# Layer 1's attention projections cut from 512-column to 256-column products

## The chip, the cores and the metric

One core of a Trainium2 chip runs the whole program. The metric is the time of one execution on the device in microseconds (us), lower is better. The kernel before takes 557.86 us, the median of three runs (557.8 to 558.06).

## What is computed

Two transformer layers over 256 tokens of width 1024, in float32. Layer 0 mixes tokens by multi-head latent attention, layer 1 by block attention (with 256 tokens there is one block, so it is plain causal attention with a relative bias). Each is followed by an MLP with squared ReLU. Cut to what matters here:

```python
def moba_mixer(h, w_qkv, q_norm, k_norm, w_o, positions, rel_bias_table):
    B, S, _ = h.shape
    qkv = (h @ w_qkv).reshape(B, S, 3, MOBA_HEADS, MOBA_HEAD_DIM)   # 256 x 1024 times 1024 x 3072
    q = rms_norm(qkv[:, :, 0], q_norm).transpose(0, 2, 1, 3)
    k = rms_norm(qkv[:, :, 1], k_norm).transpose(0, 2, 1, 3)
    v = qkv[:, :, 2].transpose(0, 2, 1, 3)
    out = moba_attention(q, k, v, positions, rel_bias_table)
    return out.transpose(0, 2, 1, 3).reshape(B, S, MOBA_HEADS * MOBA_HEAD_DIM) @ w_o

# for i in range(DEPTH):
#     x = x + mixer(rms_norm(x, attn_norm[i]))
#     h = rms_norm(x, mlp_norm[i]);  a = relu(h @ w_in);  x = x + (a * a) @ w_out
```

## The kernel before

**Products in three parts.** Every large matrix product is made of three TensorE products of type float32r: high part times high part, low times high, high times low. Activations and weights are both split so. For the hidden state the parts are hTh and hTl, for the attention output aT0 and aT1, for the MLP's inner activations a0 and a1, for weights wh and wl. Heads and transposes are products of plain float32, the bias sums of layer 1 are bfloat16; the text calls both "of another type".

**Weights.** The weights come in 185 units of 128 x 1024 numbers, in one fixed order. SyncE loads a unit into one of four raw buffers, ScalarE casts it to wh (line 169), VectorE subtracts to get wl (line 178); wh and wl each have a ring of seven buffers. Units are split ahead of use by calls that stand by hand in the program: `hi` casts the next unit, `lo` makes the next wl, `fill` does one lo and then one hi. `done(i)` says that the program is past unit i. `hi` leaves its call out, without a word, where the unit would be more than seven ahead, and `lo` where there is no wh to work on; `unit(i)` makes up for what is missing at the moment it is asked for:

```python
    def hi(n=1, eng=nc.scalar):
            if i < min(used[0] + RING, len(units)):
    def lo(n=1, eng=nc.vector):
            if i < len(his):
    def unit(i):
        while len(los) <= i:
            lo()
    def done(i):
        used[0] = max(used[0], i + 1)
```

The order of the program is written by hand, and each engine runs its own instructions in that order.

**The projections of layer 1.** There are six names (k0, q0, v0, k1, v1, q1: key, query and value for heads 0 to 3 and 4 to 7), each with four units (k0 has units 89 to 92, q0 93 to 96, v0 97 to 100, and so on) and a result for each of two token tiles t. `proj1(name, t)` is one row of work: for each of eight k, three products with 128 columns of hTh or hTl standing still and 512 columns of wh or wl moving, 24 in all. k0 runs both t together, 48 products. Between rows stand transposes of finished tiles, and later the heads.

**The wide product.** In a stretch where products of another type came before, the next suitable product of the MLPs takes 258 columns in place of 256 (`wider`; the two more columns land beside the result and are not read). In the heads, `col(d, hh)` makes output row d of the attention's last projection, heads hh; there the product (d, h) = (5, 0) is the wide one. `run_heads` calls `col(4, ...)` in pieces between the heads, and rows 5 to 7 at the end.

Of the kernel before, what the change touches and what calls it, by code (L numbers as in the profile page):

```python
# [18 lines left out]
P = 128  # L19
# [4 lines left out]
S = 256  # L24
NT = S // P
KD = D // P
H = 8
# [33 lines left out]
def trunk(ctx: ExitStack, tc: tile.TileContext, A, out):  # L61
# [9 lines left out]
    def ps():  # L71
        return psum.tile([P, 512], F32, name="ps", tag="ps")
# [11 lines left out]
    def mm(o, a, b, start, stop):  # L84
        nc.tensor.matmul(o, a, b, start=start, stop=stop)  # L85

    def mm3(o, a, b, start, stop, wide=None, between=None):

        for i, (w, t) in enumerate(((0, 0), (1, 0), (0, 1))):
            if wide and i == 0:  # L90
                mm(wide[0], a[w], wide[1], start, False)
            else:
                mm(o, a[w], b[t], start and i == 0, stop and i == 2)
            if between and between[0] == i:
                between[1]()
# [7 lines left out]
    def wider(bank, b):  # L103
        moved[0] = True
        return bank[:, :S + 2], flat(b[:, :2])[:, :S + 2]
# [8 lines left out]
    def flat(ap):  # L114
        return ap.rearrange("p a b -> p (a b)")
# [20 lines left out]
    Q0 = len(units)  # L136
# [24 lines left out]
    def hi(n=1, eng=nc.scalar):  # L161

        for _ in range(n):
            i = len(his)
            if i < min(used[0] + RING, len(units)):
                load_raw()
                w = units[i][1]
                his.append(wsp.tile([P, 1024], F32R, name="wh", tag="wh"))
                (eng.copy if eng is nc.scalar else eng.tensor_copy)(his[i][:, :w], raws[i][:, :w])  # L169

    def lo(n=1, eng=nc.vector):

        for _ in range(n):
            i = len(los)
            if i < len(his):
                w = units[i][1]
                los.append(wsp.tile([P, 1024], F32R, name="wl", tag="wl"))
                eng.tensor_sub(los[i][:, :w], raws[i][:, :w], f32(his[i][:, :w]))  # L178
                load_raw()

    def fill(n=1):
        lo(n)
        hi(n)
# [7 lines left out]
    def unit(i):  # L191
        while len(his) <= i:
            hi()
        while len(los) <= i:
            lo()
        return his[i], los[i]

    def done(i):

        used[0] = max(used[0], i + 1)  # L200

    def part(u, sl):
        return u[0][:, sl], u[1][:, sl]
# [6 lines left out]
    x = const.tile([P, KD, S], F32)  # L210
# [72 lines left out]
    def hT(k, sl=slice(None)):  # L283
        return hTh[:, k, sl], hTl[:, k, sl]

    class SumSquares:


        def __init__(self):
            self.tot = work.tile([P, 2, S], F32, name="ssum", tag="ssum", bufs=1)  # L290
            self.prev = None
# [38 lines left out]
    class Norm:  # L330
# [19 lines left out]
        def rows(self, tok):  # L350
            self.y = t2(self.nh, self.width)
            nc.vector.scalar_tensor_tensor(self.y, self.p.rearrange("p (a b) -> p a b", b=self.width), tok,
                                           self.rs[:, :, None].to_broadcast([P, self.nh, self.width]),
                                           op0=OP.mult, op1=OP.mult)
# [201 lines left out]
    class Head:  # L556


        def __init__(self, hd, aT, h, bias, extra=None):
            self.aT = (aT[0][:, h], aT[1][:, h])  # L560
            self.two = aT[0][:, :2]
            self.i = h % HG
            self.hd = hd[h // HG]
            self.h, self.bias, self.extra = h, bias, extra
# [28 lines left out]
        def turn(self):  # L593
            pt = ps()
            for i in range(3):
                nc.tensor.transpose(pt[:, i * P:(i + 1) * P], self.p[:, i * P:(i + 1) * P], ident)  # L596
            self.pT = work.tile([P, 3 * P], F32, name="pT", tag="pT", bufs=3)
            nc.scalar.copy(self.pT, pt[:, :3 * P])
# [15 lines left out]
    def out_residual(a, d, gname):  # L614
        nc.vector.tensor_add(x[:, d], a, x[:, d])
        make_h_filled(d, gname)

    def run_heads(hs, proj, post, rows, turn, mid, base, gname, n1):

        A_ = [h.logits for h in hs]  # L620
        W_ = [h.weights for h in hs]
        B_ = [h.turn for h in hs]
        C_ = [h.values for h in hs]
        accs = []

        def o(h, ds=range(4)):
            u = unit(base + h // 2)
            for d in ds:
                if h == 0:
                    accs.append(ps()[:, :S])  # L630
                c = (h % 2) * 512 + d * P
                mm3(accs[d], part(u, slice(c, c + P)), hs[h].aT, h == 0, h == H - 1)
                if h == H - 1:
                    out_residual(accs[d], d, gname)
            if h % 2:
                done(base + h // 2)

        late = {}

        def col(d, hh):  # L640
            if d not in late:
                late[d] = ps()
            u = unit(base + d)
            for h in hh:
                mm3(late[d][:, :S], part(u, slice(h * P, (h + 1) * P)), hs[h].aT, h == 0, h == H - 1,
                    wider(late[d], hs[h].two) if (d, h) == (5, 0) else None)
            if hh[-1] == H - 1:
                done(base + d)
                out_residual(late[d][:, :S], d, gname)

        if mid is not None:
            proj("k1", 0)
            fill(n1)
            post("k1", 0)
            mid()
            proj("k1", 1)
            lo(n1)
            rows("k1", 0)
            hi(n1)
            post("k1", 1)  # L660
        A_[0]()
        proj("v1", 0)
        if mid is not None:
            lo(n1)
            rows("k1", 1)
        W_[0]()
        hi(n1)
        post("v1", 0)
        turn("k1", 0)
        A_[1]()  # L670
        if mid is None:
            rows("k1", 1)
        B_[0]()
        proj("v1", 1)
        lo(n1 + (mid is None))
        W_[1]()
        hi(n1)
        post("v1", 1)
        turn("k1", 1)
        C_[0]()  # L680
        A_[2]()
        B_[1]()
        proj("q1", 0)
        lo(n1)
        W_[2]()
        hi(n1)
        post("q1", 0)
        C_[1]()
        A_[3]()
        B_[2]()  # L690
        proj("q1", 1)
        lo(n1)
        W_[3]()
        rows("q1", 0)
        hi(n1)
        post("q1", 1)
        C_[2]()
        B_[3]()
        o(0)
        fill()  # L700
        turn("q1", 0)
        rows("q1", 1)
        C_[3]()
        o(1)
        fill()
        turn("q1", 1)
        o(2, range(2))
        A_[4]()
        o(2, range(2, 4))
        W_[4]()  # L710
        A_[5]()
        lo()
        o(3)
        B_[4]()
        hi()
        W_[5]()
        A_[6]()
        col(4, [0, 1])
        C_[4]()
        B_[5]()  # L720
        W_[6]()
        A_[7]()
        lo()
        col(4, [2, 3])
        C_[5]()
        B_[6]()
        hi()
        W_[7]()
        o(4)
        fill()  # L730
        C_[6]()
        B_[7]()
        o(5)
        fill()
        C_[7]()
        o(6)
        fill()
        col(4, [4, 5, 6])
        o(7)
        col(4, [7])  # L740
        for d in range(5, KD):
            col(d, range(H))
# [9 lines left out]
    open_p = {}  # L752
# [80 lines left out]
    heads_ctx, hd, aT = head_tiles(0)  # L833
# [16 lines left out]
    for o, a, b in rope_halves(m[:, :, 0], m[:, :, 1]):  # L850
        a, b = (i[:, :, None, :].to_broadcast([P, NT, 2, HALF]) for i in (a, b))
# [221 lines left out]
    for i, bs in enumerate(pairs):  # L1073
        at = 5 * i + 9
# [13 lines left out]
    order1 = {"k0": 0, "q0": 1, "v0": 2, "k1": 3, "v1": 4, "q1": 5}  # L1088
# [18 lines left out]
        tk = slice(t * P, (t + 1) * P)  # L1107
        to_T(norms[name, t].y, hd1[int(name[1])][name[0]][:, :, tk], gqk[:, 1:2] if name[0] == "q" else None)

    def proj1_k(name, t, p, k):  # L1110
        b = Q0 + 4 * order1[name]
        tk = slice(t * P, (t + 1) * P)
        mm3(p, hT(k, tk), part(unit(b + k // 2), slice((k % 2) * 512, (k % 2 + 1) * 512)), k == 0, k == KD - 1)

    def proj1(name, t):
        p = ps()
        for k in range(KD):
            proj1_k(name, t, p, k)
        if t == NT - 1:
            done(Q0 + 4 * order1[name] + 3)  # L1120
        open_p[name, t] = p

    for t in range(NT):
        open_p["k0", t] = ps()
    for k in range(KD):
        for t in range(NT):
            proj1_k("k0", t, open_p["k0", t], k)
        if k % 2:
            fill()
            done(Q0 + k // 2)  # L1130
    total = sums1[0].total()
    for t in range(NT):
        post1("k0", t, False)
    proj1("q0", 0)
    ss3 = small.tile([P, 1, NT], F32, name="ss3", bufs=1)
    tok_sums(ss3, [total], ps())
# [100 lines left out]
```

## Time and profile before

| what | value |
|---|---|
| median of three runs | 557.86 us |
| profiled execution, its own time | 557.87 us |
| its span (first to last instruction) | 556.1 us |
| TensorE busy (PE) | 551.3 us, 99% of the span |
| VectorE busy (DVE) | 394.4 us, 71% |
| ScalarE busy (ACT) | 303.3 us, 55% |
| granted clock of TensorE | 0.999 |

The span is what the profiler saw of the program; the 1.8 us between span and time lie around it. PE busy counts a product from its start to its modelled end, and ends overlap with the next start, so the pace of products is read from starts, not from busy time. The chain that ended last names the engine that was waited for: here TensorE holds 96% of it.

### The profile page before, as it was taken

To read this page: it belongs to the slowest core of one execution; us is meant where nothing else is said; L and a number is where in the kernel's file an instruction comes from. 1 tells how busy PE (TensorE), PEld (TensorE's weight loads), DVE (VectorE), ACT (ScalarE), POOL (GpSimd) and SP (SyncE) were. 2 spreads that over 40 slices of the span, in tenths; PEclk is the share of its full clock that TensorE was granted. 3 is DMA by queue.
4 is the path that set the end of the run, shared out by engine and by line. 5 is a ranking of instruction groups with operands and counts; after the bars stand their busy time and mean duration, and the time that the engine had idled before them with its cause. 6 is when DMAs were issued, how large, how long until landed. Compare 5 with 4: busy or idle time off the path is not lost.

```text
span 556.1 us, 10756 instructions
## 1 busy us (share of the span) xinstructions
PE 551.3 (99%) x4324; PEld 525.2 (94%) x4324; DVE 394.4 (71%) x654; ACT 303.3 (55%) x495; POOL 94.1 (17%) x108
## 2 busy tenths in 40 slices
PE   9999999999999999999999999999999999999997
PEld 7878999999999999999988888999999999999997
DVE  5997777687997689866668456767867653977630
ACT  6989675674533365435365465746856432655420
POOL 4892100032132000011133100000130311000100
PEclk9999999999999999999999999999999999999999
DMA  8833545586566466645456544453865764675810
GB/s 303 298 125 114 152 128 151 194 273 196 183 198 213 118 223 195 193 158 177 156 185 186 189 155 143 123 152 116 285 206 182 237 193 146 188 202 179 273 42 29
DMA packets 29186, 99.57 MB, mean 179 GB/s; under 512 B 3824, under 2 KB 4720, under 8 KB 29136
## 3 DMA queue, kind: packets, MB, share of 16 engines
q1 hardware_dynamic: 28656, 97.94, 55.4%
q0 software_dynamic: 336, 0.92, 0.4%
q8 instruction: 34, 0.56, 0.4%
q14 instruction: 16, 0.13, 0.1%
q10 hardware_dynamic: 144, 0.02, 0.0%
HBM read 97.82 MB, written 1.05 MB: 178 GB/s over the span
## 4 chain that ended last, share of the span: by engine, by line
PE 96%; DMA 2%; SPq 1%; issue 0%; DVE 0%; ACT 0%
PE ps L85 93%; PE ps L372 2%; DMA xs<-in_x_tok 1%; PE ps L596 1%; DMA win<-in_w_in 1%; SPq L158 0%; SPq L230 0%; PE ps L512 0%; DVE wl L178 0%; ACT wh L169 0%; DVE t L1063 0%; ACT sqj L477 0%; PE ps L879 0%
## 5 line engine op out<-in xcount | busy, mean ns | idle before, releaser
L178 DVE TENSOR_TENSOR wl<-raw,wh 128x1024 fp32r<-128x1024 f32 x177 | 218.3, 1249 | 34.5 <-ACT wh L169 33.9
L169 ACT CAST wh<-raw 128x1024 fp32r<-128x1024 f32 x177 | 182.8, 1047 | 71.7 <-PE ps L85 54.1
L85 PE MATMUL ps<-a,wh 128*128 128x256 f32 x1024 | 175.0, 276 | 0.0
L85 PEld LDWEIGHTS ps<-a,wh 128*128 128x128 f32 x1024 | 154.4, 188 | 0.0
L85 PE MATMUL ps<-hTl,wh 128*128 128x256 f32 x512 | 141.7, 277 | 0.0
L85 PE MATMUL ps<-a,wl 128*128 128x256 f32 x512 | 141.7, 277 | 0.0
L85 PE MATMUL ps<-hTh,wl 128*128 128x256 f32 x512 | 141.4, 276 | 0.0
L85 PE MATMUL ps<-hTh,wh 128*128 128x256 f32 x512 | 141.3, 276 | 0.0
L85 PEld LDWEIGHTS ps<-hTh,wh 128*128 128x128 f32 x512 | 96.1, 188 | 0.1
L85 PEld LDWEIGHTS ps<-hTl,wh 128*128 128x128 f32 x512 | 96.1, 188 | 0.1
L85 PEld LDWEIGHTS ps<-a,wl 128*128 128x128 f32 x512 | 96.1, 188 | 0.0
L85 PEld LDWEIGHTS ps<-hTh,wl 128*128 128x128 f32 x512 | 96.1, 188 | 0.0
L930 ACT ACTIVATE t<-ps 128x512 f32<-128x512 f32 (+1 forms) x34 | 19.5, 573 | 63.4 <-PE ps L85 63.4
L85 PE MATMUL ps<-aT,wh 128*128 128x256 f32 (+1 forms) x256 | 50.4, 288 | 0.0
L932 DVE SCALAR_TENSOR_TENSOR t<-ps,t 128x512 f32<-128x512 f32 (+1 forms) x34 | 22.4, 659 | 36.4 <-ACT t L930 36.2
L85 PE MATMUL ps<-wh,hTh 128*128 128x512 f32 (+2 forms) x128 | 46.5, 389 | 0.3 <-ACT wh L169 0.3
L85 PE MATMUL ps<-wl,hTh 128*128 128x512 f32 (+2 forms) x128 | 45.0, 377 | 0.1
L85 PE MATMUL ps<-wh,hTl 128*128 128x512 f32 (+2 forms) x128 | 44.8, 376 | 0.0
L85 PEld LDWEIGHTS ps<-aT,wh 128*128 128x128 f32 x256 | 40.4, 188 | 0.2
L85 PE MATMUL ps<-aT,wl 128*128 128x256 f32 x128 | 35.6, 278 | 0.0
L609 ACT ACTIVATE hTh<-x,gains 128x256 fp32r<-128x256 f32 x24 | 12.2, 510 | 42.3 <-POOL x L1054 25.8
L270 POOL TENSOR_TENSOR hrs<-hss,mhalf 128x4 f32<-128x4 f32 (+1 forms) x18 | 23.2, 1298 | 65.5 <-DVE hss L347 48.8
(167 smaller groups left out, 624.4 us busy)
## 6 DMA issues: line engine op xcount, KB each, us to landing
raw<-in_w_in_mlp SPq DMA_DIRECT2D x64, 512.0 KB, 4.3
raw<-in_w_out_mlp SPq DMA_DIRECT2D x64, 512.0 KB, 4.4
raw<-in_w_qkv SPq DMA_DIRECT2D x24, 512.0 KB, 4.0
raw<-in_w_u SPq DMA_DIRECT2D x8, 512.0 KB, 6.0
win<-in_w_in SPq DMA_DIRECT2D x8, 352.0 KB, 5.2
raw<-in_w_o0a SPq DMA_DIRECT2D x4, 512.0 KB, 3.9
raw<-in_w_o0b SPq DMA_DIRECT2D x4, 512.0 KB, 3.6
raw<-in_w_o1a SPq DMA_DIRECT2D x4, 512.0 KB, 4.0
```

The costliest lines, as they stand in the source:

```text
L85: nc.tensor.matmul(o, a, b, start=start, stop=stop)
L169: (eng.copy if eng is nc.scalar else eng.tensor_copy)(his[i][:, :w], raws[i][:, :w])
L178: eng.tensor_sub(los[i][:, :w], raws[i][:, :w], f32(his[i][:, :w]))
L270: nc.gpsimd.tensor_tensor(dst, t, mhalf[:, :n].rearrange("p (a b) -> p a b", b=t.shape[-1]) if len(t.shape) == 3 else mhalf[:, :n], op=OP.pow)
L372: nc.tensor.transpose(pt[:, i * P:(i + 1) * P], yf[:, i * P:(i + 1) * P], ident)
L596: nc.tensor.transpose(pt[:, i * P:(i + 1) * P], self.p[:, i * P:(i + 1) * P], ident)
L609: nc.scalar.activation(hTh[:, k], x[:, k], AF.Copy, scale=gain(gname, k))
L930: nc.scalar.activation(rl, src, AF.Relu)
L932: nc.vector.scalar_tensor_tensor(sq, src, 0.0, rl, op0=OP.max, op1=OP.mult)
```

## The change

`proj1` now runs a row through `proj1_row`. Each 512-column product becomes two of 256 columns with the same standing operand, 48 in a row (96 for k0). Of the two halves of one product, number (k, i) = (3, 1), the first is made 258 columns wide and put in the seventh place; the other has the 254 columns that are left, and goes to the end of the row. For k0 `done` is now called after 24 and after 96 products, where before it was called after each two k. In `run_heads` the wide product goes from (5, 0) to (4, 0) and (4, 5), in both layers.

```diff
-            self.two = aT[0][:, :2]
+            self.two = aT[0][:, h:h + 2] if h < H - 1 else None
...
-                    wider(late[d], hs[h].two) if (d, h) == (5, 0) else None)
+                    wider(late[d], hs[h].two) if d == 4 and h in (0, 5) else None)
...
-    def proj1_k(name, t, p, k):
-        b = Q0 + 4 * order1[name]
-        tk = slice(t * P, (t + 1) * P)
-        mm3(p, hT(k, tk), part(unit(b + k // 2), slice((k % 2) * 512, (k % 2 + 1) * 512)), k == 0, k == KD - 1)
+    def proj1_row(todo):
+        first = todo[0]
+        kick, rest = first[:2] + (3, 1, 0), first[:2] + (3, 1, 1)
+        todo = [x for x in todo if x not in (kick, rest)]
+        todo = todo[:6] + [kick] + todo[6:] + [rest]
+        last = {x[:2]: x for x in todo}
+        for x in todo:
+            name, t, k, i, half = x
+            c0, c1 = (0, S + 2) if x == kick else (S + 2, 2 * S) if x == rest else (half * S, (half + 1) * S)
+            w = unit(Q0 + 4 * order1[name] + k // 2)[i // 2][:, (k % 2) * 512 + c0:(k % 2) * 512 + c1]
+            mm(open_p[name, t][:, c0:c1], hT(k, slice(t * P, (t + 1) * P))[i % 2], w, (k, i, half) == (0, 0, 0),
+               x == last[name, t])
+            yield
...
-    for k in range(KD):
-        for t in range(NT):
-            proj1_k("k0", t, open_p["k0", t], k)
-        if k % 2:
+    row = [("k0", t, k, i, half) for k in range(KD) for t in range(NT) for i in range(3) for half in range(2)]
+    for at, _ in enumerate(proj1_row(row), 1):
+        if at % 24 == 0:
             fill()
-            done(Q0 + k // 2)
+            if at in (24, 96):
+                done(Q0 + at // 24 - 1)
```

What this does to the order on VectorE shows between the rows q0 and v0. The names are buffers: wl_3813, wl_3857 and wl_3903 are the low parts of units 98, 99 and 100; that of unit 97 was made earlier, while k0 ran. Before:

```order
L178 TENSOR_TENSOR wl_3813<-raw_3669,wh_3760 128x1024
L343 TENSOR_REDUCE hss_3820<-t2_3819 128x4
L347 TENSOR_SCALAR hss_3820<-hss_3820,sq3_3805 128x4
L352 SCALAR_TENSOR_TENSOR t2_3851<-ps_3692,rs_3_3803,hrs_3807 128x512
L352 SCALAR_TENSOR_TENSOR t2_3853<-ps_3693,rs_3_3803,hrs_3810 128x512
L352 SCALAR_TENSOR_TENSOR t2_3855<-ps_3771,rs_3_3803,hrs_3823 128x512
L178 TENSOR_TENSOR wl_3857<-raw_3722,wh_3817 128x1024
L343 TENSOR_REDUCE hss_3866<-t2_3865 128x4
L347 TENSOR_SCALAR hss_3866<-hss_3866,sq3_3805 128x4
L178 TENSOR_TENSOR wl_3903<-raw_3740,wh_3861 128x1024
```

In the changed kernel wl_3943, wl_3947, wl_3998 and wl_4014 are the low parts of units 97, 98, 99 and 100:

```order
L343 TENSOR_REDUCE hss_3882<-t2_3881 128x4
L347 TENSOR_SCALAR hss_3882<-hss_3882,sq3_3869 128x4
L352 SCALAR_TENSOR_TENSOR t2_3937<-ps_3692,rs_3_3867,hrs_3871 128x512
L352 SCALAR_TENSOR_TENSOR t2_3939<-ps_3693,rs_3_3867,hrs_3874 128x512
L352 SCALAR_TENSOR_TENSOR t2_3941<-ps_3811,rs_3_3867,hrs_3885 128x512
L178 TENSOR_TENSOR wl_3943<-raw_3639,wh_3877 128x1024
L178 TENSOR_TENSOR wl_3947<-raw_3669,wh_3879 128x1024
L343 TENSOR_REDUCE hss_3956<-t2_3955 128x4
L347 TENSOR_SCALAR hss_3956<-hss_3956,sq3_3869 128x4
L178 TENSOR_TENSOR wl_3998<-raw_3746,wh_3951 128x1024
L178 TENSOR_TENSOR wl_4014<-raw_3776,wh_3953 128x1024
```

Two low parts have moved from ahead of the three scalings of line 352 to behind them, so that all four units of v0 get theirs after these scalings.

On TensorE, this is the start of the first row of v0 in the changed kernel (the row's result is ps_3974):

```order
L85 MATMUL ps_3974<-wh_3877,hTh_156 128x256 [waits Activation_49]
L85 MATMUL ps_3974<-wh_3877,hTh_156 128x256
L85 MATMUL ps_3974<-wh_3877,hTl_157 128x256 x2
L85 MATMUL ps_3974<-wl_3943,hTh_156 128x256 [waits DVE_49]
L85 MATMUL ps_3974<-wl_3943,hTh_156 128x256
L85 MATMUL ps_3974<-wh_3879,hTl_157 128x258 [waits Activation_49]
L85 MATMUL ps_3974<-wh_3877,hTh_156 128x256 x2
L85 MATMUL ps_3974<-wh_3877,hTl_157 128x256 x2
L85 MATMUL ps_3974<-wl_3943,hTh_156 128x256 x2
```

The same place before:

```order
L372 MATMUL ps_3878<-ident_139,t2_3853 128x128 x4
L85 MATMUL ps_3884<-wh_3742,hTh_156 128x512
L85 MATMUL ps_3884<-wh_3742,hTl_157 128x512
L85 MATMUL ps_3884<-wl_3756,hTh_156 128x512
L85 MATMUL ps_3884<-wh_3742,hTh_156 128x512
L85 MATMUL ps_3884<-wh_3742,hTl_157 128x512
L85 MATMUL ps_3884<-wl_3756,hTh_156 128x512
L85 MATMUL ps_3884<-wh_3760,hTh_156 128x512
```

Each product has become two, the fifth of the row is the first that reads a low part, and the seventh is the wide one.

## Rows read from the trace of the kernel before

**Rows 1.** The page: engine, busy us (share of the span), instructions.

```profile
PE 551.3 (99%) x4324; PEld 525.2 (94%) x4324; DVE 394.4 (71%) x654; ACT 303.3 (55%) x495; POOL 94.1 (17%) x108
```

**Rows 2.** The chain in order of time, layer 1's projections: start us, us, what.

```profile
295.27 5.60 PE ps L85 x24
...
301.31 11.20 PE ps L85 x48
```

**Rows 3.** TensorE's timeline, layer 0's last output rows: start us, us, what.

```profile
80.71 0.36 PE L85 MATMUL ps<-aT,wh 128*128 128x256 f32 x1
80.91 0.28 PE L85 MATMUL ps<-aT,wl 128*128 128x256 f32 x1
...
84.80 0.28 PE L85 MATMUL ps<-aT,wl 128*128 128x256 f32 x1
```

**Rows 4.** TensorE's timeline, an MLP's second half, two of its products.

```profile
240.12 0.28 PE L85 MATMUL ps<-a,wl 128*128 128x256 f32 x1
...
244.88 0.28 PE L85 MATMUL ps<-a,wl 128*128 128x256 f32 x1
```

**Rows 5.** TensorE's timeline from a wide product of the MLP on.

```profile
131.73 0.28 PE L85 MATMUL ps<-hTh,wh 128*128 128x258 f32 x1
...
131.97 0.28 PE L85 MATMUL ps<-hTl,wh 128*128 128x256 f32 x1
...
132.54 0.28 PE L85 MATMUL ps<-hTh,wl 128*128 128x256 f32 x1
```

**Rows 6.** Groups by form on TensorE: the wide products, count, busy us, mean ns.

```profile
L85 PE MATMUL ps<-a,wh 128*128 128x258 f32 x4 | 1.1, 280 | 0.0
...
L85 PE MATMUL ps<-hTh,wh 128*128 128x258 f32 x3 | 0.8, 280 | 0.0
...
L85 PE MATMUL ps<-aT,wh 128*128 128x258 f32 x2 | 0.6, 280 | 0.0
```

**Rows 7.** TensorE's timeline where k0's row begins.

```profile
271.40 0.39 PE L85 MATMUL ps<-wh,hTh 128*128 128x512 f32 x1
...
272.33 0.40 PE L85 MATMUL ps<-wh,hTl 128*128 128x512 f32 x1
```

**Rows 8.** TensorE's timeline from the end of q0's first row to v0.

```profile
288.19 0.50 PE L85 MATMUL ps<-ones,ssum 128*128 128x2 f32 x4
...
294.24 1.03 PE L372 MATMUL ps<-ident,t 128*128 128x128 f32 x8
295.03 0.48 PE L85 MATMUL ps<-wh,hTh 128*128 128x512 f32 x1
```

**Rows 9.** VectorE's timeline there; in brackets its idle time before and the releaser.

```profile
294.46 0.75 DVE L352 SCALAR_TENSOR_TENSOR t<-ps,rs,hrs 128x512 f32<-128x512 f32 x1 [0.23 <-POOL hrs L270]
295.12 1.22 DVE L178 TENSOR_TENSOR wl<-raw,wh 128x1024 fp32r<-128x1024 f32 x1
296.26 0.68 DVE L343 TENSOR_REDUCE hss<-t 128x4 f32<-128x512 f32 x1
296.98 0.23 DVE L347 TENSOR_SCALAR hss<-hss,sq 128x4 f32<-128x4 f32 x1
297.11 1.22 DVE L178 TENSOR_TENSOR wl<-raw,wh 128x1024 fp32r<-128x1024 f32 x1
```

**Rows 10.** ScalarE's timeline at k0's end.

```profile
279.48 4.03 ACT L169 CAST wh<-raw 128x1024 fp32r<-128x1024 f32 x4
```

**Rows 11.** The chain in order of time, near the start: VectorE hands over to TensorE.

```profile
17.74 0.90 DVE wl L178
...
18.69 1.29 PE ps L85 x7
```

**Rows 12.** VectorE's timeline in the later rows, with its idle time.

```profile
313.17 0.69 DVE L343 TENSOR_REDUCE hss<-t 128x4 f32<-128x512 f32 x1 [5.86 <-ACT t L342]
...
320.62 2.35 DVE L178 TENSOR_TENSOR wl<-raw,wh 128x1024 fp32r<-128x1024 f32 x2
```

**Rows 13.** TensorE's timeline: v1's first row begins.

```profile
318.84 0.59 PE L85 MATMUL ps<-wh,hTh 128*128 128x512 f32 x1
```

More of the change, by code (lines that the diff above doesn't have):

```diff
@@ L1108, in turn1 @@
         to_T(norms[name, t].y, hd1[int(name[1])][name[0]][:, :, tk], gqk[:, 1:2] if name[0] == "q" else None)
-    def proj1_k(name, t, p, k):
-        b = Q0 + 4 * order1[name]
-        tk = slice(t * P, (t + 1) * P)
-        mm3(p, hT(k, tk), part(unit(b + k // 2), slice((k % 2) * 512, (k % 2 + 1) * 512)), k == 0, k == KD - 1)
+    def proj1_row(todo):
[11 more added lines that the diff above has]
+            yield
     def proj1(name, t):
-        p = ps()
-        for k in range(KD):
-            proj1_k(name, t, p, k)
+        open_p[name, t] = ps()
+        for _ in proj1_row([(name, t, k, i, half) for k in range(KD) for i in range(3) for half in range(2)]):
+            pass
         if t == NT - 1:
             done(Q0 + 4 * order1[name] + 3)
-        open_p[name, t] = p
     for t in range(NT):
         open_p["k0", t] = ps()
-    for k in range(KD):
-        for t in range(NT):
-            proj1_k("k0", t, open_p["k0", t], k)
-        if k % 2:
+    row = [("k0", t, k, i, half) for k in range(KD) for t in range(NT) for i in range(3) for half in range(2)]
+    for at, _ in enumerate(proj1_row(row), 1):
+        if at % 24 == 0:
             fill()
-            done(Q0 + k // 2)
+            if at in (24, 96):
+                done(Q0 + at // 24 - 1)
     total = sums1[0].total()
```

## The prediction

> **What bounds the kernel now.** I read the page first: TensorE is busy for 551.3 of 556.1 us [rows 1], so time is won only by a faster pace of its products, or lost by a wait put in front of it. Then the chain in order of time, for the pace of the part that is changed: 24 products of 512 columns take 5.60 us, 48 take 11.20, so 233.3 ns each, row after row [rows 2]. Then TensorE's timeline, start against start, for the pace of 256 columns. There are two. In the last rows of layer 0, behind the heads, 33 products lie between the two wl rows shown (of three products one reads wl): 84.80 - 80.91 = 3.89 us, 117.8 ns each [rows 3]. In the MLP 42 products lie between them: 4.76 us, 113.3 ns each [rows 4]. Same columns, same type, and a granted clock of 0.999 over the whole run. What changes the one pace into the other is seen at a wide product: it starts at 131.73, and from 131.97 to 132.54 five products take 0.57 us, 114 ns each [rows 5]. All nine wide products of the kernel [rows 6] are followed by the quick pace two products later; before them, back to the last product of another type, it is the slow one. So 512 columns cost 233.3 ns as one product, 226.7 as two quick ones, 235.6 as two slow ones.
>
> **Term 1, the projections' pace.** There are 288 products of 512 columns (k0 48, ten rows of 24), 67.2 us. They become 576. A single row starts behind transposes or heads, so slow: six products, then the wide one and the one after it, then 40 quick ones: 8 x 0.1178 + 40 x 0.1133 = 5.474 us against 5.600, a gain of 0.126; ten rows, 1.26 us. k0 follows the MLP's quick products directly, but the quick pace is gone at once when its operands come: four products from 271.40 to 272.33, 232.5 ns each [rows 7]. I treat it as a row that starts slow: 8 x 0.1178 + 88 x 0.1133 = 10.91 against 11.20, a gain of 0.29. Together -1.55 us. No row of before shows 256 columns with a weight moving and the hidden state standing, which is the reverse of the MLP. The bounds are therefore the two paces: 576 x 0.1133 = 65.3 us (-1.9) and 576 x 0.1178 = 67.9 (+0.7). I take the side of the quick one, because nine wide products of nine worked, with three different moving tiles; that they all had a weight standing is the reason to keep the other end.
>
> The Trainium skill speaks against this edit: TensorE: Matmul & The Clock Gate, Back-to-back issue gap, gives a product N / 2.4 + 2.5 ns at full clock, so that each of 288 products cut in two would pay another fixed 2.5 ns, an estimated 0.7 us more in all and nothing back. The trace agrees with neither of the levels that follow from it, 215.8 ns for 512 columns (measured 233.3) and 109.2 for 256 (113.3 or 117.8), but its fixed part is close to what two slow products cost over one, 2.3 ns.
>
> **Term 2, the wide product in the output rows.** From (4, 5) to the old place (5, 0) lie three products of head 5, three of head 6, twelve of `o(7)` and three of head 7: 21, all of type float32r, which go from 117.8 to 113.3 ns: 21 x 4.5 = 0.09 us, in two layers -0.19 us. The one at (4, 0) has five products behind it before heads of another type come: -0.02 us a layer at best; I count nothing.
>
> **Term 3, the weights come late.** k0's seventh product reads unit 90, whose other half is read last, so `done` for units 90 and 91 waits for the end of the row. Until then `hi` may go no further than unit 96. Before, k0's four `fill`s made wh and wl up to units 98 and 97; now the fourth does nothing. The next `fill(2)` casts 97 and 98, but its `lo`s find nothing to do, as wh and wl both stand at 96. So VectorE makes the low parts of 97 and 98 only at the `fill(2)` behind the three scalings of line 352, and those of 99 and 100 when v0's first row asks for them. ScalarE is no hurdle: before, it casts units 95 to 98 in one run up to 283.51 [rows 10], and even a few us later is in time.
>
> I set the clock at 288.19, the end of q0's first row [rows 8], since the norm's sums that follow feed VectorE's chain. The last scaling starts 6.27 us later, released by GpSimd (294.46) [rows 9]; this wait does not move. From there, with VectorE's own rows: scaling 0.66 (294.46 to 295.12), 97 and 98 1.14 each (295.12 to 296.26), reduction and scalar 0.85 (296.26 to 297.11), unit 99 1.22. Low part 97 is there after 6.27 + 0.66 + 1.22 = 8.15, 99 after 6.27 + 0.66 + 2.28 + 0.85 + 1.22 = 11.28 us. TensorE takes 0.05 us to start on VectorE's result (18.64 to 18.69) [rows 11].
>
> TensorE without a wait: sums and q0's second row 6.05 (to 294.24) less 0.13, transposes 0.79 (to 295.03): v0 starts at 6.71 [rows 8]. A first product of 256 columns behind another type takes 0.2 us to the next start (80.71 to 80.91) [rows 3]. The fifth product, which reads wl of unit 97, would start at 6.71 + 0.2 + 3 x 0.118 = 7.27 and waits until 8.20: 0.93 us. The 28th, first to read wl of unit 99, would start at 6.71 + 0.2 + 26 x 0.1135 = 9.86, and cannot before 11.33. The whole loss is the larger, **1.45 us**; 98 and 100 come 1.14 us after 97 and 99 and are asked for 13 and 12 products (1.4 us) after them, so add nothing. With the slow pace throughout v0 starts 0.15 later and reaches its 28th product at 10.1: 1.2 us. The bounds are 0 (if VectorE finds room earlier, for which I see no row) and 1.6. Behind the second wait 20 products may run slow, +0.05 us.
>
> No other row waits. k1: VectorE had 5.86 us of idle time there [rows 12]. v1: its low parts of 107 and 108 start where those of 108 and 109 do now, at 320.62 [rows 12]; 107 is ready at 321.9 and is read by the 28th product, no earlier than 318.84 + 0.2 + 26 x 0.1135 = 322.0 [rows 13]. That is the closest, 0.1 us to spare. By the attention's end both kernels have split the same units.
>
> **The sum.** -1.55 - 0.19 + 1.45 + 0.05 = -0.24 us on the profiled execution's 557.87 (its span 556.1 and 1.8 us around it; the median is 557.86): **557.6 us**, no change that can be told. A measurement of this kernel tells about 0.2%, 1.1 us, from no change.
>
> **The rivals.**
> - *The wait is not there* (12%): terms 1 and 2 stand alone, -1.74, 556.1 us. It decides for faster once the wait is under 0.6 us. It needs VectorE to finish unit 99 some 0.9 us earlier; the scaling that is released by GpSimd at 294.46 speaks against it.
> - *The quick pace does not come* (24%): with weights moving the wide product changes nothing, and 576 products at 117.8 ns cost +0.65; with the wait of 1.2 and the heads' -0.19 this is +1.66, 559.5 us, slower. It decides from a mean pace of 116.9 ns: 576 x 0.1169 - 67.2 + 1.2 - 0.19 = 1.1. For it: 512 columns in this arrangement never hold 226.7 ns; against it: nine of nine. The fixed part of the Trainium skill's page above leads to the same place: by its 2.5 ns, with wait and heads, an estimated 559.6.
> - *The quick pace comes in some rows, or ends at v0's wait* (14%): half of term 1's gain, -0.5 over all rows, + 1.35 - 0.19: about 558.5, still within 0.2%.
> - *The forecast* (50%): 557.2 to 558.1 by k0's row (-0.29 or +0.1) and the wait (1.2 to 1.6).
>
> So faster 0.13, same 0.63, slower 0.24. The range from 556.8 to 559.7 leaves out the first rival and a wait longer than I see; the forecast's own is 557.2 to 558.1.
>
> **What would show it.** Right: rows of 48 between transposes at about 5.47 us; starts 113 ns apart from the ninth product on; in v0's first row two idle times on TensorE of 0.9 and 0.5 us, released by VectorE's line 178; k0 near 10.9 us; rows 5 to 7 of the output unchanged, and the 21 products ahead of them at 113. Wrong: starts 118 apart behind the wide product (then 559.5), or no wait at v0 (then 556.1), or a wait in v1's first row too.

## The result, and the profile after

The changed kernel takes 565.51 us (median of four executions, 565.33 to 565.61) against 557.96 (557.80 to 558.82): a ratio of 1.0131, 95% interval 1.0118 to 1.0144. It is slower, and outside the predicted range. The page of the changed kernel (engine, busy us, share of the span, instructions), to set against [rows 1]:

```profile
span 563.8 us, 11328 instructions
...
PE 558.4 (99%) x4612; PEld 545.3 (97%) x4612; DVE 395.0 (70%) x654; ACT 302.0 (54%) x495; POOL 91.0 (16%) x108
```

TensorE has 288 products more, since 288 of 512 columns have become 576 of about half the width, and is busy 7.1 us longer. Where they lie shows in the chain of the changed kernel (start us, us, what); its pieces around layer 1's projections answer to [rows 2]:

```profile
79.25 215.10 PE ps L85 x1930
294.35 0.87 PE ps L372 x8
295.22 3.12 PE ps L85 x27
298.34 0.03 issue
298.37 2.74 PE ps L85 x21
...
301.55 11.14 PE ps L85 x96
...
364.41 196.15 PE ps L85 x1662
560.56 0.02 issue
```

and in the same places of the chain before:

```profile
78.89 215.50 PE ps L85 x1834
294.40 0.87 PE ps L372 x8
...
363.81 189.03 PE ps L85 x1662
552.84 0.02 issue
```

The two chains read against each other give the whole difference of 7.72 us in the spans. Up to 79 us the changed kernel is 0.36 late, a delay that is there at 18 us, ahead of any changed instruction. From there to the end of q0's second row it wins 0.41 (the heads' edit in layer 0, k0 and q0's first row). To 364 us it loses 0.65, some 0.45 in the other rows and 0.2 in layer 1's heads. The last piece then loses 7.12. It holds 1662 products in both kernels: 189.03 / 1662 = 113.7 ns each before, 196.15 / 1662 = 118.0 after. That is the slow pace of [rows 3] from layer 1's last heads to the end of the program, where before the quick one of [rows 4] began at 369.95. The granted clock is 1.0.

The two wide products that should have ended it ran and did not. In the second MLP, whose code the change does not touch, the wide product behind the norm's sum stands in TensorE's timeline of the changed kernel as in [rows 5], with the opposite effect:

```profile
418.15 0.59 PE L85 MATMUL ps<-ssum,ones 128*128 128x256 f32 x2
...
419.05 0.28 PE L85 MATMUL ps<-hTh,wh 128*128 128x258 f32 x1
419.17 0.28 PE L85 MATMUL ps<-hTh,wl 128*128 128x256 f32 x1
...
419.87 0.28 PE L85 MATMUL ps<-hTh,wl 128*128 128x256 f32 x1
```

From 419.17 to 419.87 lie six products, 117 ns each. [Rows 5] had 114 there.

The slow pace has a beat. Three slow products take 353 ns, which the trace gives as 117, 118 and 118, and one of each three has a duration 1 ns longer than the other two (the ends are modelled, so this is a mark of how the starts fall, no more). Groups by line and form show which one it is: count, shortest, median and longest duration in ns, first and last start. Ahead of the wide product that worked in the kernel before (369.95), the long one is always the product that reads wl, the second of each three:

```profile
L85 PE MATMUL ps<-aT,wh x23: 279/279/279, 365.9 to 369.8; 128*128 128x256 f32 x23
L85 PE MATMUL ps<-aT,wl x12: 280/280/280, 365.8 to 369.7; 128*128 128x256 f32 x12
```

Ahead of the one that failed in the changed kernel (368.09) it is never wl, but one of the two that read wh (by single products the first: 280 at 367.73, then 279 at 367.85 and 367.97):

```profile
L85 PE MATMUL ps<-aT,wh x9: 279/279/280, 366.6 to 368.0; 128*128 128x256 f32 x9
L85 PE MATMUL ps<-aT,wl x5: 279/279/279, 366.4 to 367.9; 128*128 128x256 f32 x5
```

So the long product lies two before the wide one that worked, and three before the one that failed. At 419.05 it lies one before. That is the **theory of the beat**: in a slow stretch a wide product works only when the long one lies two before it. The rivals: the **place** (4, 5) or its two columns are wrong and (5, 0) is right; or the **projections**' new form leaves something behind.

### The profile page after: what moved, and what is told of

Read it like the earlier page. It is cut to its first block, busy times and chain, and to the rows that moved or that the text cites. A ratio compares the mean times of both kernels' runs of the same rounds, so it can differ in the third digit from the quotient of the medians.

```text
span 563.8 us, 11328 instructions
## 1 busy us (share of the span) xinstructions
PE 558.4 (99%) x4612; PEld 545.3 (97%) x4612; DVE 395.0 (70%) x654; ACT 302.0 (54%) x495; POOL 91.0 (16%) x108
## 4 chain that ended last, share of the span: by engine, by line
PE 96%; DMA 2%; SPq 1%; issue 0%; DVE 0%; ACT 0%
PE ps L85 93%; PE ps L372 1%; DMA xs<-in_x_tok 1%; PE ps L596 1%; DMA win<-in_w_in 1%; SPq L158 0%; SPq L230 0%; PE ps L512 0%; DVE wl L178 0%; ACT wh L169 0%; DVE t L1064 0%; ACT sqj L477 0%; PE ps L880 0%
## 5 line engine op out<-in xcount | busy, mean ns | idle before, releaser
L85 PE MATMUL ps<-a,wh 128*128 128x256 f32 x1024 | 178.5, 278 | 0.0
L85 PE MATMUL ps<-wh,hTh 128*128 128x256 f32 (+2 forms) x224 | 46.3, 291 | 0.9 <-ACT wh L169 0.9
L85 PE MATMUL ps<-wh,hTl 128*128 128x256 f32 (+2 forms) x224 | 46.7, 285 | 0.0
L85 PE MATMUL ps<-wl,hTh 128*128 128x256 f32 (+2 forms) x224 | 45.2, 286 | 0.1
L85 PEld LDWEIGHTS ps<-wh,hTh 128*128 128x128 f32 x224 | 34.8, 189 | 1.8 <-ACT wh L169 1.2
L85 PEld LDWEIGHTS ps<-wh,hTl 128*128 128x128 f32 x224 | 35.5, 188 | 0.0
```

## The experiments

All are compared with the kernel before, run on the same chip in the same job (medians 558.3 to 558.4).

**Which part?** *heads_only* is the kernel before with the line of `col` changed and the projections as they were; *proj_only* is the changed kernel with the wide product back at its old place.

```
-  self.two = aT[0][:, :2]      # heads_only
+  self.two = aT[0][:, h:h + 2] if h < H - 1 else None
...
-  wider(late[d], hs[h].two) if (d, h) == (5, 0) else None)
+  wider(late[d], hs[h].two) if d == 4 and h in (0, 5) else None)
```

> The kernel before with the wide product of the output rows moved to (4, 0) and (4, 5) and nothing else. Beat theory (a wide product turns the slow pace into the quick one only on one of three places in the slow pace's beat): (4, 5) lies 21 products, seven beats, ahead of (5, 0), so it hits as (5, 0) did, unless the changed layer 0 moves the beat; about 557.7 us, and layer 1's MLP at 113.3 ns a product. Place theory (moving the wide product is itself what loses layer 1's MLP): about 565 us.

> The changed kernel with the wide product of the output rows back at (5, 0). Beat theory: what comes ahead of layer 1's output rows is that of the changed kernel, and (5, 0) has the same place in the beat as (4, 5), so it misses too and layer 1's MLP stays at 117.8 ns: about 565.5 us. Place theory: the MLP is quick again, about 558.3 us.

*proj_only* takes 565.42 (ratio 1.0130, 1.0115 to 1.0145): all of the loss, with the wide product at its old place. That ends the rival of the place. *heads_only* takes 557.73 to 558.97 in nine executions and 565.44 in one, the profiled one: the same program makes both times, which neither rival allows. Its profile has the failing beat ahead of the wide product:

```profile
L85 PE MATMUL ps<-aT,wh x9: 279/279/280, 366.4 to 367.8; 128*128 128x256 f32 x9
L85 PE MATMUL ps<-aT,wl x4: 279/279/279, 366.6 to 367.7; 128*128 128x256 f32 x4
```

Its instructions in layer 1 are those of before up to the wide product at 357.41, so the two can be followed to the first gap that differs. It is that of the first output product behind a head's logits in layer 1: it lasts 469 ns in the kernel before (first fence) and 467 in *heads_only* (second), while the gaps between the 800 products ahead of it agree to 1 ns.

```profile
L85 PE MATMUL ps<-aT,wh x1: 469/469/469, 353.2 to 353.2; 128*128 128x256 f32 x1
```

```profile
L85 PE MATMUL ps<-aT,wh x1: 467/467/467, 353.6 to 353.6; 128*128 128x256 f32 x1
```

Where the last stretch begins, behind the last head's values, the first product lasts 362 ns in the kernel before (first fence) and 365 in *heads_only* (second), and from there on the long one stands elsewhere:

```profile
L85 PE MATMUL ps<-aT,wh x1: 362/362/362, 365.6 to 365.6; 128*128 128x256 f32 x1
```

```profile
L85 PE MATMUL ps<-aT,wh x1: 365/365/365, 366.1 to 366.1; 128*128 128x256 f32 x1
```

This holds in all fourteen traces: where this product lasts 365 ns (nine traces, the changed kernel's among them), the long product is then the first of each three; where it lasts 362 or 363, it is the second (four traces), or there is no slow pace (one, *own_early0* below). A shift of 3 ns at an entry decides over 7 us.

**The same wide product, one or two products later.** In the changed kernel layer 1's wide product at (4, 5) becomes the second (*beat1*) or the third (*beat2*) of its three.

```
-            if wide and i == 0:
-                mm(wide[0], a[w], wide[1], start, False)
+            if wide and i == (wide[2] if len(wide) > 2 else 0):
+                mm(wide[0], a[w], wide[1], start and i == 0, stop and i == 2)
...
+                if n1 == 2 and h == 5:            # layer 1, (4, 5); beat1: hs[h].two) + (1,)
+                    return wider(late[d], hs[h].two1) + (2,)
```

> The changed kernel, in layer 1 alone the 258 columns at (4, 5) taken by the second of its three products (low weights) in place of the first. Beat theory: in the changed kernel's slow stretch the first product is one place late against the stretches where it hit, the second is two late; it misses again, about 565.5 us (or some 5 less if the MLP's own wide product at its sums happens to hit). Place theory: no difference from the changed kernel, 565.5 us.

> The changed kernel, in layer 1 alone the 258 columns at (4, 5) taken by the third of its three products (low part of the attention output moving). Beat theory: this is the place that hits; quick from there to the end of the program, 6.8 us of the MLP and 0.3 of the output rows back: about 558.4 us. Place theory, or something that the projections leave behind (ring, instruction fetch): no difference, 565.5 us.

*beat2* takes 558.44 in the median of ten executions (558.00 to 558.96; ratio 1.0003, 0.9993 to 1.0013): two products' delay gives back all 7 us, with the projections of the changed kernel, so these leave nothing behind that keeps the pace slow by itself. The beat at the entry is that of the changed kernel, and the third product has the long one two before it:

```profile
L85 PE MATMUL ps<-aT,wh x10: 279/280/280, 366.2 to 367.7; 128*128 128x256 f32 x10
L85 PE MATMUL ps<-aT,wl x5: 279/279/279, 366.4 to 367.8; 128*128 128x256 f32 x5
```

*beat1* takes 560.40 (ratio 1.0040, 1.0024 to 1.0056): the second product misses, but the MLP's own wide product, at 419.21, now works and the quick pace holds from there.

**The MLP's own wide product.** *sums_earlier* is the changed kernel with the norm's sum one product earlier in layer 1, to put the wide product a product later behind it.

```
-  between = other_type(1, lambda: mm(pb[:, :S], ones, s, True, True))
+  between = other_type(0 if l else 1, lambda: mm(pb[:, :S], ones, s, True, True))
```

> The changed kernel, with the norm's sum of layer 1's MLP one product earlier, so that its wide product (missed at 419.05 us) comes fifth instead of fourth behind the sum's row. Theory of the beat (of three slow products one lasts 1 ns longer, and a wide product works when that one lies two before it, as in every one that worked): in the changed kernel the long one was the last before the wide product, so it now lies two before. It works, 1196 products go from 117.8 to 113.3 ns, 5.4 us: 560.1. Rival, the MLP cannot be made quick after a missed wide product in the heads, or its operands no longer fit: nothing changes, 565.5. A third way, the new place of the sum shifts the beat again: also 565.5, and the durations ahead of the wide product tell it from the rival.

565.38 (ratio 1.0121, 1.0101 to 1.0142): nothing gained. The durations are 280, 279, 279 ahead of the wide product, so the beat moved with the sum, the third way of the expectation. A beat read in one version does not hold in the next.

**The control on the kernel before.** *heads_third* is *heads_only* with layer 1's wide product on the third product.

> The kernel before the change with its output rows' wide product at (4, 0) and (4, 5) (558.2 in nine executions, 565.4 in one), in layer 1 on the third product of (4, 5) instead of the first; the projections are those of before. Theory of the beat: where the first falls on it, the third doesn't: it now misses in most executions and works in few, the reverse of the other kernel. Missed, layer 1's output rows and MLP stay slow, 560.2 if the MLP's own wide product works, 565.4 if not. Rival (the third of three is simply the better place, since it worked in all ten executions with the changed projections): 558.2 in all.

The median is 565.06 (ratio 1.0092, 1.0065 to 1.0119): six of ten executions take 565.1 to 565.8, three 559.4 to 560.1, one 557.84. *heads_only* had nine of ten near 558. The third product is not the better place as such. The profiled execution is the one at 557.84, and has the beat of *beat2*.

**A wide product in a quick stretch.** *undo* is the kernel before with a second wide product in each layer, 24 products behind the one that works.

```
-  wider(late[d], hs[h].two) if (d, h) == (5, 0) else None)
+  wider(late[d], hs[h].two) if (d, h) in ((5, 0), (6, 0)) else None)
```

> The kernel before the change, with one more wide product in each layer, at (6, 0) of the output rows, 24 products behind the one at (5, 0), where the pace is quick already. Theory (a wide product in a quick stretch turns it slow): in both layers the pace is 113.3 from (5, 0) on, 117.8 from (6, 0) on, until the wide product behind the next sums: some 375 products x 4.5 ns = 1.7 us in each layer, 558.3 + 3.4 = 561.7, if the wide products there still fall on the beat; if layer 1's misses, its 1196 products add 5.4, 567.1. Rival (a wide product sets the quick pace whatever it was, and what ended it in the projections' rows is that weights move): no change, 558.3.

561.66 (ratio 1.0060, 1.0042 to 1.0077), as expected. Groups ahead of the added wide product of layer 1, and behind it:

```profile
L85 PE MATMUL ps<-aT,wh x15: 276/276/276, 372.3 to 374.7; 128*128 128x256 f32 x15
L85 PE MATMUL ps<-aT,wl x7: 276/276/276, 372.5 to 374.6; 128*128 128x256 f32 x7
...
L85 PE MATMUL ps<-aT,wh x18: 279/280/281, 375.0 to 378.0; 128*128 128x256 f32 x18
L85 PE MATMUL ps<-aT,wl x9: 279/279/281, 374.9 to 377.8; 128*128 128x256 f32 x9
```

276 is the quick pace's duration, 279 and 280 the slow one's: the wide product does not set a pace, it changes it.

**The rows without it.** The same happens in the projections. In the changed kernel seven of the eleven rows have turned quick by themselves when their seventh product comes; it is the wide one, and turns them slow. q0's first row seems to start slow for a like reason: it follows k0 directly, which is quick up to its last product, the one of 254 columns, and slow from that one on (starts 113 or 114 ns apart before, 117 to 119 after, in all ten traces with the new rows). No run leaves that product alone out. *own_pace* is *beat2* with wide products only in k0, q0's and v0's first row and k1's first; *own_pace2* leaves out k1's too.

```
-        kick, rest = first[:2] + (3, 1, 0), first[:2] + (3, 1, 1)
...
+        kick = rest = None
+        if first[:2] in (("k0", 0), ("q0", 0), ("v0", 0), ("k1", 0)):   # own_pace2: without k1
+            kick, rest = first[:2] + (3, 1, 0), first[:2] + (3, 1, 1)
...
```

> The changed kernel with layer 1's wide product at (4, 5) on its third product (558.4), and without a wide product in the seven rows where it ended a quick pace that was there already: q0's and v0's second row, k1's second, both of v1 and both of q1; their 48 products have 256 columns each. Theory (a row behind transposes or heads turns quick by itself within five products, and the wide product in a quick stretch turns it slow): these rows go from 5.72 to about 5.48 us, seven times -0.24, -1.7: 556.7, provided that the wide product at (4, 5) still falls on the beat; if it doesn't, some 6.8 more, 563.5, with the rows quick all the same. Rival (the pace of a row falls back by itself a few products on, as with 512 columns): rows of 48 x 117.8 = 5.7 us, no change, 558.4.

> As own_pace (557.4: wide product at (4, 5) on its third product, none in the seven rows that turn quick by themselves), and none in k1's first row either: there the row before is quick to its end, so k1's row begins quick and the wide product turned it slow (5.63 us). Theory: k1's first row 5.44 us, -0.19: 557.25, if the wide product at (4, 5) still works. Rival (the entry into the output rows shifts with the shorter row, as with the early splits): the third product misses, 563; or part of the executions each way.

*own_pace*: 557.44 (ratio 0.9981, 0.9972 to 0.9990); *own_pace2*: 557.20 (0.9980, 0.9971 to 0.9989). Both are 0.2% faster than the kernel before, and none of their executions (ten and eleven) is above 557.94; a miss costs 2 us (*beat1*) or more, so all kept the quick pace to the end. TensorE's timeline of q0's second row, the changed kernel first, then *own_pace*:

```profile
289.01 0.39 PE L85 MATMUL ps<-wl,hTh 128*128 128x256 f32 x2
289.24 0.28 PE L85 MATMUL ps<-wh,hTl 128*128 128x258 f32 x1
289.35 0.40 PE L85 MATMUL ps<-wh,hTh 128*128 128x256 f32 x2
...
293.83 0.40 PE L85 MATMUL ps<-wl,hTh 128*128 128x256 f32 x2
```

```profile
289.18 0.39 PE L85 MATMUL ps<-wh,hTh 128*128 128x256 f32 x2
...
293.71 0.40 PE L85 MATMUL ps<-wl,hTh 128*128 128x256 f32 x2
```

From 289.35 to 293.83 lie 38 products, 118 ns each; from 289.18 to 293.71 in *own_pace* 40, 113 each. The two products ahead of the wide one at 289.24 take 0.23 us, 115 ns each, so the row was quick already. The seven rows gain 0.18 us each, not the 0.24 that I expected, 1.26 in all. Of that 0.25 goes into v0's first row, which begins earlier and waits longer (5.90 us in *beat2*, 6.15 here), and 0.14 into k1's first, which now begins quick and was turned slow by its wide product; *own_pace2* has that back (5.63 to 5.44). That its time is the expected one is in part luck: q1's first row, which has no wide product in either, turned quick in *own_pace* and stayed slow through all its 48 products in *own_pace2* (5.54 and 5.74 us). Its products of high part times high part, by durations, first *own_pace*, then *own_pace2*:

```profile
L85 PE MATMUL ps<-wh,hTh x16: 276/276/369, 333.3 to 338.3; 128*128 128x256 f32 x16
```

```profile
L85 PE MATMUL ps<-wh,hTh x16: 281/281/365, 333.0 to 338.2; 128*128 128x256 f32 x16
```

The same row stayed slow in *own_early* and *own_early0*. All rows together are only 0.05 us shorter in the trace of *own_pace2* than in that of *own_pace*, and their two ratios do not differ clear of noise.

**v0's wait.** *early* is *beat2* with units 97 and 98 split behind k0's row; *own_early* has *own_pace*'s rows too; *own_early0* has *own_pace2*'s rows and the wide product at (4, 5) on its first product.

```
     for t in range(NT):
         post1("k0", t, False)
+    both(2)
     proj1("q0", 0)
```

> The changed kernel with the wide product at (4, 5) on its third product (558.4), and units 97 and 98 cast and split right behind k0's row instead of three rows later. Theory (v0's first row waits 0.2 us for the low part of 99 and is slow behind that wait): no wait, the row goes from 5.90 to 5.5 us, -0.4: 558.0, if (4, 5) still falls on the beat. Rival one: the splits now run beside GpSimd's powers or ahead of VectorE's norm chain, the scalings come later, and the wait stays or grows: 558.4 to 559. Rival two: the slow end of v0's row is not from the wait; the wait goes and the row stays near 5.7: 558.2.

> Both of the edits before together: no wide product in the seven rows that turn quick by themselves, and units 97 and 98 split behind k0's row. Theory: the gains add, 558.4 - 1.7 - 0.4 = 556.3, 0.36% under the kernel before the change, if the wide product at (4, 5) falls on the beat. Rival: the entry into the last rows of layer 1's attention output shifts by some ns, the wide product there misses in some executions or in all: 563 us in these.

> The changed kernel without a wide product in eight of its eleven rows (the seven that turn quick by themselves and k1's first, which now follows a quick row), with units 97 and 98 split behind k0's row, and the wide product at (4, 5) on its first product as in the change. Theory: with the early splits the long product was the last one before the third of (4, 5), so it lies two before the first: that one works. Rows quick: q0's second to v1's second near 5.5 us each, 0.15 less than in own_early in k1's; 557.4 (own_pace) - 0.5 (v0's row) - 0.15: 556.8 or a little less. Rival (the entry shifts by some ns again, since k1's row is shorter): missed, 563 to 564.

The wait goes. In the chain of *early* v0's first row is one piece of 5.51 us, where the changed kernel has two with an issue time between; start to start the row takes 5.59 us instead of 5.90 in *beat2*:

```profile
295.11 5.51 PE ps L85 x48
```

A second wait, which the prediction did not have, goes with it. Output row 4 of layer 1 reads unit 117. Its low part is made at 351.00 in the kernel before and at 356.57 in the changed one, whose splits stay one unit behind from v0's rows on. VectorE's split and the first two products of that row, before and after:

```profile
351.00 1.21 DVE L178 TENSOR_TENSOR wl<-raw,wh 128x1024 fp32r<-128x1024 f32 x1
...
356.96 0.47 PE L85 MATMUL ps<-aT,wh 128*128 128x256 f32 x1
357.26 0.28 PE L85 MATMUL ps<-aT,wl 128*128 128x256 f32 x1
```

```profile
356.57 1.22 DVE L178 TENSOR_TENSOR wl<-raw,wh 128x1024 fp32r<-128x1024 f32 x1
...
357.38 0.47 PE L85 MATMUL ps<-aT,wh 128*128 128x258 f32 x1
357.85 0.38 PE L85 MATMUL ps<-aT,wl 128*128 128x256 f32 x1
```

The product that reads the low part starts 0.47 us behind the one ahead of it instead of 0.30, once the split has ended, and the next one is 0.10 us later still. In *early* this is as before. All seven traces with this wait (the changed kernel, *proj_only*, *beat1*, *beat2*, *sums_earlier*, *own_pace*, *own_pace2*) have the 365 ns at the last stretch's entry; of the seven without it five have 362 or 363, and two, *heads_only* and *heads_third*, have 365. So in the changed kernel the late weights go together with the shifted beat, but the shift also comes without them, and no run separates this wait from v0's: that they cause it is not shown.

But the times of *early* and *own_early* are 564.78 (1.0110, 1.0093 to 1.0126) and 564.26 (1.0102, 1.0087 to 1.0117): in both the beat at layer 1's entry moved, the long product now being wl, one before the wide third:

```profile
L85 PE MATMUL ps<-aT,wh x10: 279/279/279, 365.9 to 367.4; 128*128 128x256 f32 x10
L85 PE MATMUL ps<-aT,wl x5: 280/280/280, 366.1 to 367.5; 128*128 128x256 f32 x5
```

*own_early0* spreads over three times: 556.31 to 556.58 in three executions, 558.24 to 559.09 in eight, 563.58 in one (median 558.51, ratio 1.0002, 0.9983 to 1.0021). In the profiled one, at 559.09, the last output rows are quick by themselves from 365.13 on and the wide product at 366.92 ended it, so the eight look like *undo*'s case; of the three only the times are known. 556.4 is what this program can reach, and it isn't to be had on purpose with these means.

**The count.** Over the fourteen traces (before, after and twelve experiments) 58 wide products stand in output rows or behind a norm's sum, other products of their type ahead of them. With the long product two before: 42, all worked. One or three before: 13, none worked. In a quick stretch: 3, all ended it. In the projections' rows 36 came in slow stretches, which have no such beat there (nearly all products last 281 ns), and the quick pace followed each: within four products in 26, and only from the fifth product behind in the other ten, all in v0's first row, so that there it may have come by itself. 44 came in quick stretches, and all ended them. Behind the table sums of the first MLP, 70 of 70 worked; the five products ahead of them are not yet steady, and always the same.

## Why the prediction was wrong

**Term 1** failed at "I take the side of the quick one, because nine wide products of nine worked", and at "A single row starts behind transposes or heads, so slow". The first read as a law what was one state of entry, met nine times. The second carried the output rows' and the MLP's slow starts over to rows that the trace did not show in 256 columns; of the eight rows behind transposes, sums or heads all but v0's first turned quick before their wide product. The rows that are slow when the wide product comes, and behind which no wait follows, came nearly as worked out, though none of them stands behind transposes or heads, but behind the MLP or another row: k0 11.19 to 10.93 us (-0.26, forecast -0.29), q0's first 5.60 to 5.49 and k1's first 5.60 to 5.49 (forecast -0.126). The other seven lost 0.04 to 0.06 each instead of gaining 0.126. With v0's first row (+0.29) all rows together come to +0.14 us, against -0.05 with term 3. The rival that the quick pace comes in some rows covers this, and its 558.5 is close to the 558.44 of *beat2*, where the output rows work; its half of the gain, put at 0.5, would be 0.78. It did not go on to what lies behind the projections.

**What was held unchanged** cost the most: "rows 5 to 7 of the output unchanged". No term and no rival priced a miss for the 1662 products from layer 1's last heads on, whose code the diff leaves alone but for the place of one wide product. Their pace hangs on two wide products; both missed, and 7.12 of the 7.72 us were lost there. This is the step that put the time outside the range: the quick pace there was taken as given, because the wide products had always worked.

**Term 2** was right in layer 0 (0.357 us late at 82 us, 0.263 at 86, so -0.09 as forecast), and in layer 1 the moved wide product missed. Moving it was neither enough to cause that (*heads_only* mostly hits) nor needed (*proj_only* misses).

**Term 3** was right in its place and too large: the wait is 0.19 us, not 1.45 (1.47 by its own starts, 11.33 less 9.86). The chain's 27 products from 295.22 end with the 0.03 of issue, and the 28th starts at 298.37, 0.30 us behind the one ahead of it instead of 0.11; VectorE had just ended unit 99. It was the 28th product, as forecast; the fifth did not wait. Two things were mis-sized. I held the third scaling at 6.27 us behind q0's first row; it comes after 5.22. VectorE's timeline of the changed kernel, to set against [rows 9]:

```profile
293.30 0.75 DVE L352 SCALAR_TENSOR_TENSOR t<-ps,rs,hrs 128x512 f32<-128x512 f32 x1 [0.23 <-POOL hrs L270]
293.97 2.35 DVE L178 TENSOR_TENSOR wl<-raw,wh 128x1024 fp32r<-128x1024 f32 x2
296.24 0.68 DVE L343 TENSOR_REDUCE hss<-t 128x4 f32<-128x512 f32 x1
...
297.09 2.35 DVE L178 TENSOR_TENSOR wl<-raw,wh 128x1024 fp32r<-128x1024 f32 x2
```

The scaling waits for GpSimd's three powers. GpSimd's timeline, before and after, with VectorE's row that stood beside it before:

```profile
290.42 4.00 POOL L270 TENSOR_TENSOR hrs<-hss,mhalf 128x4 f32<-128x4 f32 x3 [0.54 <-DVE hss L347]
...
290.38 1.22 DVE L178 TENSOR_TENSOR wl<-raw,wh 128x1024 fp32r<-128x1024 f32 x1
```

```profile
290.31 2.96 POOL L270 TENSOR_TENSOR hrs<-hss,mhalf 128x4 f32<-128x4 f32 x3 [0.54 <-DVE hss L347]
```

Three powers take 2.96 us alone and 4.00 beside one split: the first of them, which starts 0.04 us behind the split, takes 2.08 us, the others 1.00 and 1.01. The edit that made the weights late took that split away from them, and so paid 1.04 us of the wait. The Trainium skill says this (SBUF — State Buffer, SBUF: two separate sides): an operation of VectorE with two inputs in SBUF and one of GpSimd that reads SBUF exclude each other for a whole instruction; the trace agrees, with 1.04 us lost beside a split of 1.22. My sentence "this wait does not move" had the releaser right and did not ask what the releaser itself waited for. The second is a later demand: q0's second row was slow (5.74 us, 5.55 by the forecast), and v0's row quick only from its 12th product, not its 9th, so the 28th was asked for 0.24 us later.

The forecast that no other row of the projections waits held. "By the attention's end both kernels have split the same units" did not: the changed kernel is one unit behind, and pays with the second wait, 0.17 us at 357.85 and 0.10 behind it. The argument from the Trainium skill's page TensorE: Matmul & The Clock Gate (Back-to-back issue gap) had the direction, slower, by luck and not by its mechanism: the same 1662 products cost 113.7 or 118.0 ns in the mean, where a fixed part for each allows only one value, and a quick row of 48 products takes 5.54 us in *own_pace*, where the 24 took 5.68.

**Still open:** what the beat is in the engine, why only products with weights standing have it, and what moves the first product of a stretch by 3 ns, by the times in all executions of the changed kernel and in one of ten of *heads_only*. The late weights of the changed kernel are one candidate; *heads_only* shows a shift without them, where none of the 800 products ahead of it differs.

## What to carry to other kernels

A device that worked each time in a trace may have met the same state each time: before a prediction rests on it, look for what would make it fail, and price what lies behind it to its next chance, in code that the diff does not touch as well. Where a change shifts starts by some ns ahead of such a device, its effect can be the same in every execution (the changed kernel) or a draw in each (*heads_only*, *heads_third*, *own_early0*): compare many, and read the single times, not the median alone. When a wait is released by another engine, ask also what slows that engine, and whether the edit removes it.

## What the runs showed of the hardware

- At a full granted clock, products of 256 columns of type float32r have two stable paces, 113.3 and 117.8 ns. A product of 258 columns changes from one to the other in either direction. In stretches with a weight standing the slow pace has a beat of three, and the change to quick needs one place of it.
- With a weight standing, what a wide product leaves behind it follows from what it met. After it has ended a quick stretch (three cases), a long product stands fifth behind it, and then each third. After a miss one stands sixth, if the long product was three before the wide one (five cases), or fourth, if it was one before (eight cases). So the four states, quick and three places of the beat, go over into four different states, and no row of added wide products brings all of them to quick. The cases are from the traces; the conclusion was not run.
- A projection's row of 256 columns behind transposes, sums or heads mostly turns quick by itself, most often within some five products. Of seven such rows in each of ten traces 67 of 70 did; q1's first row stayed slow to its end in three. The eighth, v0's first, was still slow at its seventh product in all ten. The last output rows of layer 1 were quick by themselves in one trace of fourteen.
- GpSimd's power of 128 x 4 takes some 1.0 us, and 2.08 when it starts just behind a split of VectorE (1.22 us).
